# Hybrid attention block on one core: the projections between the heads as a stream of single products

## The chip, the cores and the metric

The kernel runs on one core of one Trainium2 chip. The metric is the device time of one execution in microseconds (us), the median of several runs. TensorE (PE in the profile) multiplies, VectorE (DVE), ScalarE (ACT) and GpSimd (POOL) work on rows, SyncE (SP) issues most transfers; each engine takes its instructions in a fixed order.

## The reference, cut to what matters

Two layers, each of an attention part and an MLP, on 512 rows of width 1024. In the attention part one normalised input `h` is projected, the projections go through four kinds of heads with four heads each, and the sixteen outputs go through `w_out`.

```
h = rmsnorm(x, norm_mix_g[l]) * (1.0 + sc1) + sh1
z = h @ w_in[l]
za, zb, zc, zd = split_last(z, [SWA_COLS, MLA_COLS, NSA_COLS, MOBA_COLS])
o = concatenate([swa_mixer(za), mla_mixer(zb), nsa_mixer(zc), moba_mixer(zd)])
x = x + g1 * (o @ w_out[l])
h = rmsnorm(x, norm_mlp_g[l]) * (1.0 + sc2) + sh2
x = x + g2 * (square(relu(h @ w_up[l])) @ w_down[l])
```

SWA is attention in a band of 128 keys with two key heads and a sink, MLA is causal attention over low-rank projections, NSA adds a compressed branch to two causal branches (at 512 rows all its blocks are chosen), MoBA is causal here too. Everything is in float32 and the output must agree with it.

## The kernel before, in words

**Products in three.** A float32 product is made of three single products of rounded operands (`fp32r`): weight high by input high, weight high by input low, weight low by input high (lines 363 to 369). The high part of a weight (`whi`, line 87) is made on ScalarE, the low part (`wlo`, line 91) on GpSimd. The class `Weights` hands weights out in the order in which they were added: `get` loads up to three weights ahead into four `raw` buffers (DMAs on SP), and splits up to three ahead into four pairs of buffers.

**Projections.** `proj_T` (line 394) makes one projection of 128 columns by 512 rows: for each of 8 blocks of depth three products of 512 columns into one PSUM bank, 24 in all, then an evacuation. `proj_N` (line 543) makes the values with the rows on the partitions: for MoBA (`proj_VB`) four banks, each of 24 products of 256 columns. A query evacuation (`q_evac`, line 506) is two copies on ScalarE and two subtractions on VectorE; a key evacuation (`k_evac`, line 519) is four copies on ScalarE (lines 525 and 526), two subtractions on VectorE and two copies on GpSimd.

**Heads.** `softmax` (line 581) takes four blocks of 128 queries: score products into one of two banks (`sc`), a fused add-and-minimum on VectorE (line 596), the exponential on ScalarE (line 601), the reciprocal, and the normalisation, for block 0 on GpSimd (lines 573, 575), for the others on ScalarE or VectorE. The rest of a head, its `tail`, is put on the list `pending` and traced by `flush` after the softmax of the next head. In the tail `pv` (line 616) transposes ten blocks of 128x128 (seven in an SWA head) on TensorE (line 626) in three groups of 4, 4 and 2 into PSUM tiles `pt`, of which there are two buffers. Each group is split into `ph` on ScalarE (line 448) and `pl` on VectorE (line 449), and then eight value products add into `po` (lines 641, 642).

**Order.** The heads come as four of MLA, eight of NSA (four heads, two branches), four of MoBA, four of SWA. Between the MLA heads stand two query projections of NSA (lines 869 and 913). Between the NSA and MoBA heads the list `fills` (lines 975 to 991) hands one closed projection to each head: the two key and two query projections of MoBA, its values, three empty places, then the key and two query projections of SWA. The output products (`px`) with `w_out` follow, and each may begin with the heads that are done.

The program order is no queue order. A planner reads the whole program, keeps a priority in program order, and gives each engine, by its own estimate of when an operand is ready, the first instruction that can go; so products of a later projection fill places where earlier work waits. `tc.issue_after(ins)` bars an instruction from being placed ahead of `ins` on its engine. `ada_step` puts one row product of the modulation on VectorE (line 191) and one load on SP behind each head, through the same `raw` buffers.

Of the kernel before, what the change touches and what calls it, by code (L numbers as in the profile page):

```python
# [11 lines left out]
F32R = mybir.dt.float32r  # L12
# [5 lines left out]
P = 128  # L18
S = 512
D = 1024  # L20
KT = D // P
# [7 lines left out]
NSTART = 5  # L29
# [80 lines left out]
def layer_stack(ctx: ExitStack, tc: tile.TileContext, a, out):  # L110
# [341 lines left out]
    def attention_layer(l, n1, finish):  # L452
# [25 lines left out]
        with ExitStack() as es:  # L478
# [79 lines left out]
                return ws  # L558


            pending = []

            def flush():
# [52 lines left out]
            def pv(po, vsrc, p, banks, first, last):  # L616

                prods = []
                for bi, bank in enumerate(banks):
                    pt = psT.tile([P, 512], F32, tag="pt", name="pt")  # L620
                    c = 0
                    spans = []
                    for j, qs in bank:
                        c0 = c
                        for n, col in qs:
                            nc.tensor.transpose(  # L626
                                pt[:, c : c + P], p[n][:, col : col + P], ident
                            )
                            c += P
                        spans.append((j, qs[0][0], c0, c))  # L630
                    wide = 256 if c <= 256 else 512
                    ph = sp.tile([P, wide], F32R, tag=f"ph{wide}", name=f"ph{bi}")[:, 0:c]
                    pl = sp.tile([P, wide], F32R, tag=f"pl{wide}", name=f"pl{bi}")[:, 0:c]
                    split(ph, pl, pt[:, 0:c])
                    for j, n0, c0, c1 in spans:
                        prods.append((j, n0 * P, ph[:, c0:c1], pl[:, c0:c1]))
                for i, (j, q0, ph, pl) in enumerate(prods):
                    w = ph.shape[1]
                    end = last and i == len(prods) - 1
                    dst, vhl = po[:, q0 : q0 + w], vsrc(j)  # L640
                    nc.tensor.matmul(dst, vhl, ph, start=(first and i == 0), stop=False)
                    nc.tensor.matmul(dst, vhl, pl, start=False, stop=end)
# [217 lines left out]
            mla_v(2)  # L860
            if l:
                proj_T(hs, [kcvc_evac])
            mla_head(1)
            ada_step(1, last["dve"])
            with tc.issue_after(last["dve"].ins):
                nc.vector.tensor_scalar_add(gates, gates, 1.0)
                nc.vector.reciprocal(gates, gates)
            if l or NSTART < 6:
                proj_T(hs, [q_evac(nq, 0)])

            cw2 = qp.tile([P, 192], F32, tag="cw2", name="cw2")
            nc.sync.dma_start(cw2, a["cw2"][l])
# [19 lines left out]
            for kv in range(2):  # L892
                nc.tensor.matmul(
                    hps[:, 32 * kv : 32 * kv + 32], hsb[:, kv * P : (kv + 1) * P], csum,
                    start=True, stop=True,
                )
            mla_head(2)
            ada_step(1, last["dve"])
            hx = qp.tile([P, 2, 31], F32, tag="hx", name="hx")
# [10 lines left out]
            nc.gpsimd.memset(grep, 0.0)  # L910
            nc.vector.tensor_copy(grep[:, :, 0:31], hx[:, 1:2, :].to_broadcast([P, 4, 31]))
            mla_q(3)
            proj_T(hs, [q_evac(nq, 1)])
            cps = mmbank("cmpkv")
            nc.tensor.matmul(cps[:, 0:31], cw2[:, 0:128], hx[:, 0, :], start=True, stop=True)
            nc.tensor.matmul(cps[:, 64:128], grep, cw2[:, 128:192], start=True, stop=True)
# [19 lines left out]
            split(vc[:, :, 0, :], vc[:, :, 1, :], vcf)  # L936

            biasN = [bias_tile("biasN", 0), bias_tile("biasN", 2)]
            mla_head(3)
            ada_step(1, last["dve"])  # L940

# [28 lines left out]
            nc.vector.tensor_tensor(ce_, ce_, cd.unsqueeze(2).to_broadcast([P, 16, 32]), op=ALU.mult)  # L970


            mq, mk, sq_, sk = {}, {}, {}, {}
            biasM, biasS = [], []
            fills = []

            def fill():
                if fills:
                    fills.pop(0)()

            def proj_VB():
                VB.append(xp.tile([P, NQ, 4, 2, 64], F32R, tag="V", name="VB"))
                proj_N(256, 4, lambda j, ps: v_evac(VB[0], j, ps, 4))

            VB = []
            for f in (k_evac(mk, 0), k_evac(mk, 1), q_evac(mq, 0), q_evac(mq, 1)):
                fills.append(lambda f=f: proj_T(hs, [f]))
            fills.append(proj_VB)
            fills += [lambda: None] * 3
            for f in (k_evac(sk, 0), q_evac(sq_, 0), q_evac(sq_, 1)):  # L990
                fills.append(lambda f=f: proj_T(hs, [f]))
            for h in range(4):
                pos_ = {}
                for br in range(2):
                    kh, kl = nk[br]

                    def scores(n, ps, kh=kh, kl=kl, h=h):
                        w = P * (n + 1)
                        qs = slice(n * P, n * P + P)
                        nc.tensor.matmul(ps, nq[h][:, qs], kh[:, 0:w], start=True, stop=False)  # L1000
                        nc.tensor.matmul(ps, nq[h][:, qs], kl[:, 0:w], start=False, stop=True)

                    gcol = 4 * (br + 1) + h
                    p = softmax(
                        scores, causal_w, rel(biasN[h // 2][:, h % 2, :]), -1.0, BIGPOS,
                        ("gate", lambda n, c=gcol: gates[:, n, c : c + 1]),
                    )
                    flush()

                    if h == br == 0:  # L1010
                        pct = psT.tile([P, 512], F32, tag="pt", name="pct")
                        for n in range(NQ):
                            nc.tensor.transpose(
                                pct[:, n * P : (n + 1) * P],
                                ce_[:, 4 * n : 4 * n + 4, :].rearrange("p h c -> p (h c)"), ident,
                            )
                        pch = mp.tile([P, S], F32R, tag="m", name="pch", bufs=8)
                        pcl = mp.tile([P, S], F32R, tag="m", name="pcl", bufs=8)
                        split(pch, pcl, pct)

                    def tail(h=h, br=br, p=p, pos_=pos_):
                        if br == 0:
                            pos_["po"] = psO.tile([P, 512], F32, tag="po", name="po")
                        po = pos_["po"]
                        pv(
                            po, lambda j: VA[:, j, 2 + br, :, :],
                            p, causal_banks, br == 0, False,
                        )
                        if br == 1:
                            nc.tensor.matmul(po, vc[:, h, :, :], pcl, start=False, stop=False)  # L1030
                            nc.tensor.matmul(po, vc[:, h, :, :], pch, start=False, stop=True)
                            o_evac(po, 2, h)
                            if h % 2:
                                o_done(4 + h // 2)
                    pending.append(tail)
                    fill()
                    ada_step(1, last["dve"])
                if h % 2:
                    biasM.append(bias_tile("biasM", h - 1))


            for h in range(4):
# [15 lines left out]
                    if h % 2:  # L1058
                        o_done(6 + h // 2)
                pending.append(tail)  # L1060
                fill()
                ada_step(1, last["dve"])
                if h == 1:
                    biasS.append(bias_tile("biasS", 0, 4, 256))


            nsink = smp.tile([P, 4], F32, tag="nsink", name="nsink")
# [325 lines left out]
```

## Time and profile before

| what | value |
|---|---|
| median of three runs | 1287.53 us (1287.36 to 1289.71) |
| the profiled execution | 1289.0 us |
| its span, first to last instruction | 1287.2 us |
| busy TensorE, VectorE, ScalarE, GpSimd | 97%, 53%, 45%, 42% |
| mean granted TensorE clock | 0.981 |
| attention heads, layer 0 and layer 1 | about 75 to 263 us, about 700 to 882 us |

A matmul's row in the trace gives its start and a modelled end that reaches over the start of the next one; the distance between two starts is what one of them costs. A bracket at the end of a row is the idle time of the engine before it and what ended it.

### The profile page before, as it was taken

The numbers are of one execution on the slowest core, as the hardware profiler recorded it, in microseconds if no ns is written. First come the engines' busy times: TensorE is split into PE (matmuls) and PEld (weight loads), VectorE is DVE, ScalarE is ACT, GpSimd is POOL, SyncE is SP. The second block draws the span as 40 slices with busy tenths as digits, with TensorE's granted clock in tenths as the row PEclk, the third lists the DMA queues.
The fourth block names the chain that finished last, engine by engine and source line by source line (L and its number), as shares of the span: only waits on it lengthen the run. The fifth ranks groups of instructions, "written<-read, shape, count | busy, mean of one in ns | idle before, by whom it ended". The sixth has DMA issues, their size and how long they took to land. (4 is left out here: it accounts for less than half of the span.)

```text
span 1287.2 us, 17945 instructions
## 1 busy us (share of the span) xinstructions
PE 1245.9 (97%) x6572; PEld 1042.1 (81%) x6572; DVE 681.3 (53%) x1498; ACT 583.4 (45%) x1121; POOL 545.8 (42%) x495
## 2 busy tenths in 40 slices
PE   5989999989999999999999999999999999999997
PEld 4878787879888888888899778778988888888887
DVE  5758867976455554553255685895543223123124
ACT  5557767744442231331245675884443223223120
POOL 5423323454645445445425432334364444444430
PEclk7989999999999999999999999999999999999998
DMA  9645324452366756655334411313142233323312
GB/s 339 246 118 164 115 72 142 148 201 90 120 191 204 243 183 224 222 182 199 126 110 140 135 43 57 99 58 107 50 131 89 93 98 98 98 85 95 99 33 66
DMA packets 53128, 171.02 MB, mean 133 GB/s; under 512 B 6192, under 2 KB 9776, under 8 KB 53040
## 3 DMA queue, kind: packets, MB, share of 16 engines
q1 hardware_dynamic: 51312, 165.67, 39.5%
q10 hardware_dynamic: 1728, 4.20, 1.0%
q8 instruction: 52, 0.85, 0.3%
q14 instruction: 36, 0.29, 0.1%
HBM read 163.29 MB, written 4.19 MB: 130 GB/s over the span
## 5 line engine op out<-in xcount | busy, mean ns | idle before, releaser
L91 POOL TENSOR_TENSOR wlo<-raw,whi 128x512 fp32r<-128x512 f32 (+3 forms) x372 | 488.2, 1337 | 560.8 <-ACT whi L87 525.3
L87 ACT ACTIVATE whi<-raw 128x1024 fp32r<-128x1024 f32 (+3 forms) x186 | 193.8, 1046 | 459.2 <-PE px L368 249.0
L368 PE MATMUL pj<-hlo,whi 128*128 128x512 f32 (+1 forms) x768 | 288.0, 376 | 0.0
L367 PE MATMUL pj<-hhi,whi 128*128 128x512 f32 (+1 forms) x768 | 287.1, 376 | 0.0
L369 PE MATMUL pj<-hhi,wlo 128*128 128x512 f32 (+1 forms) x768 | 287.1, 374 | 0.0
L367 PE MATMUL px<-a,whi 128*128 128x512 f32 (+2 forms) x584 | 214.9, 368 | 0.0
L368 PE MATMUL px<-a,whi 128*128 128x512 f32 (+2 forms) x584 | 214.7, 368 | 0.0
L369 PE MATMUL px<-a,wlo 128*128 128x512 f32 (+2 forms) x584 | 214.6, 368 | 0.0
L411 DVE SCALAR_TENSOR_TENSOR x<-px,mod,x 128x512 f32<-128x512 f32 (+2 forms) x95 | 62.7, 665 | 199.2 <-PE px L369 199.2
L369 PEld LDWEIGHTS pj<-hhi,wlo 128*128 128x128 f32 x768 | 144.9, 189 | 26.7
L368 PEld LDWEIGHTS pj<-hlo,whi 128*128 128x128 f32 x768 | 145.1, 189 | 26.1
L367 PEld LDWEIGHTS pj<-hhi,whi 128*128 128x128 f32 x768 | 144.1, 188 | 26.1
L191 DVE CUSTOM_DVE_ANT_0 adaw<-cb,adaw,vecs 128x1024 f32<-128x1024 f32 x78 | 102.0, 1307 | 50.7 <-DMA adaw<-in_wadaD 50.7
L368 PEld LDWEIGHTS px<-a,whi 128*128 128x128 f32 x584 | 109.7, 188 | 19.7
L367 PEld LDWEIGHTS px<-a,whi 128*128 128x128 f32 x584 | 109.7, 188 | 19.7
L369 PEld LDWEIGHTS px<-a,wlo 128*128 128x128 f32 x584 | 109.7, 188 | 19.7
L1134 DVE SCALAR_TENSOR_TENSOR t<-pj,r 128x512 f32<-128x512 f32 x64 | 44.1, 691 | 148.0 <-ACT r L1133 147.8
L449 DVE TENSOR_TENSOR a<-t,a 128x512 fp32r<-128x512 f32 x64 | 81.8, 1280 | 41.9 <-ACT a L448 41.9
L601 ACT ACTIVATE e<-e,nm 128x128 f32<-128x128 f32 (+5 forms) x160 | 85.9, 539 | 10.3 <-DVE nm L596 9.8
L449 DVE TENSOR_TENSOR pl<-pt,ph 128x512 fp32r<-128x512 f32 (+1 forms) x112 | 64.8, 597 | 5.9 <-ACT ph L448 5.1
L626 PE MATMUL pt<-ident,e 128*128 128x128 f32 x376 | 60.9, 276 | 4.3 <-POOL e L573 3.8
L448 ACT ACTIVATE ph<-pt 128x512 fp32r<-128x512 f32 (+1 forms) x112 | 56.0, 524 | 13.5 <-PE pt L626 12.2
(237 smaller groups left out, 1806.6 us busy)
## 6 DMA issues: line engine op xcount, KB each, us to landing
adaw<-in_wadaD SPq DMA_DIRECT2D x78, 512.0 KB, 4.4
raw<-in_wup SPq DMA_DIRECT2D x64, 512.0 KB, 3.6
raw<-in_wdown SPq DMA_DIRECT2D x64, 512.0 KB, 3.5
raw<-in_winT SPq DMA_DIRECT2D x28, 512.0 KB, 3.8
ada<-in_wadaP SPq DMA_DIRECT2D x16, 512.0 KB, 8.9
raw<-in_wout SPq DMA_DIRECT2D x16, 512.0 KB, 3.5
cw<-in_cw SPq DMA_DIRECT2D x4, 512.0 KB, 5.0
raw<-in_cw SPq DMA_DIRECT2D x4, 512.0 KB, 4.8
```

The lines of the kernel that those rows point to most:

```text
L87: self.nc.scalar.activation(vh[0:rows], raw[0:rows], AF.Copy)
L91: eng.tensor_tensor(lo[0:rows, c], flat[0:rows, c], hi[0:rows, c].bitcast(F32), op=ALU.subtract)
L191: last["ada"] = nc.vector.tensor_tensor_reduce(out=w, in0=cv, in1=w, scale=1.0, scalar=vecs[:, off : off + 1], op0=ALU.mult, op1=ALU.add, ...
L367: nc.tensor.matmul(ps, wh[:, k, :], hh[:, c], start=first, stop=False)
L368: nc.tensor.matmul(ps, wh[:, k, :], hl[:, c], start=False, stop=False)
L369: nc.tensor.matmul(ps, wl[:, k, :], hh[:, c], start=False, stop=last)
L411: last["dve"] = nc.vector.scalar_tensor_tensor(X["x"][m][:, c], ps, mod[l][:, part, m : m + 1], X["x"][m][:, c], op0=ALU.mult, op1=ALU.add)
L448: nc.scalar.activation(hi, src, AF.Copy)
L449: last["dve"] = nc.vector.tensor_tensor(lo, src, hi.bitcast(F32), op=ALU.subtract)
L601: nc.scalar.activation(ee, ee, AF.Exp, bias=nm[:, n : n + 1], scale=-1.0, accum_out=den[:, n : n + 1])
L626: nc.tensor.transpose(pt[:, c : c + P], p[n][:, col : col + P], ident)
L1134: nc.vector.scalar_tensor_tensor(t, ps, 0.0, r, op0=ALU.max, op1=ALU.mult)
```

## The change

The two query projections between the MLA heads and all projections of `fills` are no longer closed loops. `stream_T` and `stream_N` put their products one by one on a list, each with its number of columns; the first product of a bank draws the weight and the bank, the last one evacuates it. `pull` traces the next product. In `pv` each transposition is followed by one `pull`, and that product is tied behind the transposition by `issue_after`. After each NSA and MoBA head `fill(share)` traces untied products until the head's share is spent; `share` is a twelfth of all columns, 9216, the products pulled in `pv` count against it. `drain` traces what is left. The stream for the heads is made up before the last MLA head, so ten of its products are pulled there, and the three empty places are gone. What is computed stays the same.

```diff
@@ in attention_layer
+            stream, spent = [], [0.0, 0.0]
+            def pull(behind=None):
+                if not stream:
+                    return
+                cols, begin, product, end = stream.pop(0)
+                spent[0] += cols
+                if begin is not None:
+                    begin()
+                if behind is None:
+                    product()
+                else:
+                    with tc.issue_after(behind.ins):
+                        product()
+                if end is not None:
+                    end()
+            def drain():
+                while stream:
+                    pull()
+            def fill(cols):
+                spent[1] += cols
+                while stream and spent[0] < spent[1]:
+                    pull()
+            def stream_T(evac):
+                st = {}
+                def begin():
+                    st["w"], st["ps"] = W.get(), mmbank("pj")
+                for k in range(KT):
+                    for i, (a_, b_) in enumerate(((0, 0), (0, 1), (1, 0))):
+                        def product(k=k, i=i, a_=a_, b_=b_):
+                            nc.tensor.matmul(
+                                st["ps"], st["w"][a_][:, k, :], hs[k][b_],
+                                start=(k + i == 0), stop=(k == KT - 1 and i == 2),
+                            )
+                        stream.append((
+                            S, begin if k + i == 0 else None, product,
+                            (lambda: evac(st["ps"])) if k == KT - 1 and i == 2 else None,
+                        ))
+            def stream_N(ncols, step, evac):
+                st = {}
+                def begin(j):
+                    if j == 0:
+                        st["ws"] = [W.get() for _ in range(-(-KT // step))]
+                    st["ps"] = mmbank("pn")
+                for j in range(NQ):
+                    js = slice(j * P, (j + 1) * P)
+                    for k in range(KT):
+                        for i, (a_, b_) in enumerate(((0, 0), (0, 1), (1, 0))):
+                            def product(k=k, i=i, a_=a_, b_=b_, js=js):
+                                nc.tensor.matmul(
+                                    st["ps"][:, 0:ncols], hs[k][a_][:, js],
+                                    st["ws"][k // step][b_][:, k % step, :],
+                                    start=(k + i == 0), stop=(k == KT - 1 and i == 2),
+                                )
+                            stream.append((
+                                ncols, (lambda j=j: begin(j)) if k + i == 0 else None, product,
+                                (lambda j=j: evac(j, st["ps"])) if k == KT - 1 and i == 2 else None,
+                            ))
...
                         for n, col in qs:
-                            nc.tensor.transpose(
+                            pull(nc.tensor.transpose(
                                 pt[:, c : c + P], p[n][:, col : col + P], ident
-                            )
+                            ))
...
+            if l or NSTART < 6:
+                stream_T(q_evac(nq, 0))
             mla_head(1)
...
-            if l or NSTART < 6:
-                proj_T(hs, [q_evac(nq, 0)])
+            drain()
...
+            stream_T(q_evac(nq, 1))
             mla_head(2)
...
             mla_q(3)
-            proj_T(hs, [q_evac(nq, 1)])
+            drain()
...
+            mq, mk, sq_, sk = {}, {}, {}, {}
+            VB = []
+            def vb_evac(j, ps):
+                if j == 0:
+                    VB.append(xp.tile([P, NQ, 4, 2, 64], F32R, tag="V", name="VB"))
+                v_evac(VB[0], j, ps, 4)
+            for f in (k_evac(mk, 0), k_evac(mk, 1), q_evac(mq, 0), q_evac(mq, 1)):
+                stream_T(f)
+            stream_N(256, 4, vb_evac)
+            for f in (k_evac(sk, 0), q_evac(sq_, 0), q_evac(sq_, 1)):
+                stream_T(f)
+
+            share = sum(t[0] for t in stream) / 12
+            spent[:] = [0.0, 0.0]
             mla_head(3)
...
-            for f in (k_evac(mk, 0), k_evac(mk, 1), q_evac(mq, 0), q_evac(mq, 1)):
-                fills.append(lambda f=f: proj_T(hs, [f]))
-            fills.append(proj_VB)
-            fills += [lambda: None] * 3
-            for f in (k_evac(sk, 0), q_evac(sq_, 0), q_evac(sq_, 1)):
-                fills.append(lambda f=f: proj_T(hs, [f]))
...
-                    fill()
+                    fill(share)
...
-                fill()
+                fill(share)
...
+            drain()
```

## Rows read from the trace of the kernel before

**Rows 1.** The head of the page and its first part: busy time, share of the span and number of instructions by engine.

```profile
span 1287.2 us, 17945 instructions
PE 1245.9 (97%) x6572; PEld 1042.1 (81%) x6572; DVE 681.3 (53%) x1498; ACT 583.4 (45%) x1121; POOL 545.8 (42%) x495
```

**Rows 2.** Busy time by stretch: the stretch, its length, busy us of PE, PEld, DVE, ACT and POOL with the number of instructions, the granted clock of TensorE, the share of the DMA engines, GB/s. The first two are the heads of layer 0 from the first NSA head on, the fourth the NSA heads of layer 1, the third and the fifth are the MLP stages.

```profile
119.00:193.00 74.00, 71.82 (x427) 60.64 (x426) 57.56 (x182) 53.25 (x130) 18.68 (x22) 1.00 0.30 92
193.00:232.00 39.00, 36.32 (x185) 29.01 (x183) 31.59 (x90) 29.45 (x71) 15.04 (x14) 0.96 0.46 150
...
300.00:672.00 372.00, 371.01 (x1804) 308.91 (x1804) 186.34 (x284) 120.04 (x168) 179.13 (x134) 1.00 0.54 177
...
745.00:810.00 65.00, 63.07 (x371) 52.17 (x371) 45.31 (x141) 44.10 (x105) 20.35 (x22) 1.00 0.16 51
...
920.00:1287.00 367.00, 359.39 (x1711) 297.39 (x1711) 108.14 (x158) 107.73 (x146) 155.84 (x124) 0.99 0.27 86
```

**Rows 3.** The waits of TensorE over the whole span: what waited, for whom, us in total, times, the longest.

```profile
PE po L641 <- ACT ph L448: 6.5, 13, 2.3
...
PE pt L626 <- POOL e L573: 3.8, 1, 3.8
...
PE px L367 <- ACT ohi L448: 1.5, 1, 1.5
```

**Rows 4.** The timeline of TensorE around four transpositions in a run (first four rows) and around a single one between products of 512 columns (last three rows): start, us, line, operation, how many were merged.

```profile
132.01 0.39 PE L1001 MATMUL sc<-kl,q 128*128 128x512 f32 x1
132.24 0.60 PE L626 MATMUL pt<-ident,e 128*128 128x128 f32 x4
...
132.91 0.40 PE L369 MATMUL pj<-hhi,wlo 128*128 128x512 f32 x1
133.14 0.40 PE L367 MATMUL pj<-hhi,whi 128*128 128x512 f32 x1
...
90.35 0.40 PE L842 MATMUL sc<-mkh,mql 128*128 128x512 f32 x1
90.58 0.27 PE L626 MATMUL pt<-ident,e 128*128 128x128 f32 x1
...
90.92 0.39 PE L368 MATMUL pj<-hlo,whi 128*128 128x512 f32 x1
```

**Rows 5.** The MoBA heads of layer 0: the timeline of TensorE (first three rows), of ScalarE (two rows), and the stretch at the lower clock (columns as in Rows 2).

```profile
210.56 0.50 PE L641 MATMUL po<-ph,VB 128*128 128x512 f32 x1 [2.30 <-ACT ph L448]
...
213.17 0.63 PE L368 MATMUL pj<-hlo,whi 128*128 128x512 f32 x1
213.59 0.63 PE L369 MATMUL pj<-hhi,wlo 128*128 128x512 f32 x1
...
204.27 1.06 ACT L87 ACTIVATE whi<-raw 128x1024 fp32r<-128x1024 f32 x1 [1.72 <-DMA raw<-in_wout]
...
209.91 1.09 ACT L448 ACTIVATE ph<-pt 128x512 fp32r<-128x512 f32 x2
...
212.10:215.50 3.40, 3.40 (x13) 2.92 (x11) 1.62 (x3) 0.70 (x2) 0.00 (x0) 0.50 0.76 193
```

**Rows 6.** The end of the heads of layer 0: the timeline of TensorE (two rows), and the group of the first third of the output products between 73 and 263 us (line, engine, operation, shape, count, busy us, mean ns, idle before).

```profile
265.98 1.20 PE L367 MATMUL px<-ohi,whi 128*128 128x512 f32 x4 [1.55 <-ACT ohi L448]
...
269.94 0.50 PE L369 MATMUL px<-ohi,wlo 128*128 128x512 f32 x1 [0.49 <-POOL wlo L91]
...
L367 PE MATMUL px<-ohi,whi 128*128 128x512 f32 x28 | 11.2, 405 | 0.2
```

**Rows 7.** The timeline of TensorE in the NSA heads of layer 1, from the second transposition group to the third.

```profile
768.32 0.71 PE L626 MATMUL pt<-ident,e 128*128 128x128 f32 x5
768.78 0.48 PE L367 MATMUL pj<-hhi,whi 128*128 128x512 f32 x1
...
772.27 0.39 PE L367 MATMUL pj<-hhi,whi 128*128 128x512 f32 x1
773.19 0.50 PE L641 MATMUL po<-ph,VA 128*128 128x512 f32 x1 [0.52 <-ACT ph L448]
...
774.22 0.38 PE L626 MATMUL pt<-ident,e 128*128 128x128 f32 x2
```

**Rows 8.** The timeline of ScalarE in the same stretch: the split of a weight, the first and the last of the four copies of a key evacuation, and the split of the transposed blocks.

```profile
766.42 1.06 ACT L87 ACTIVATE whi<-raw 128x1024 fp32r<-128x1024 f32 x1 [1.39 <-PE pj L368]
767.38 0.58 ACT L525 ACTIVATE kh<-pj 64x512 fp32r<-64x512 f32 x1
...
770.21 0.60 ACT L526 ACTIVATE kh<-pj 64x512 fp32r<-64x512 f32 x1
...
772.54 1.08 ACT L448 ACTIVATE ph<-pt 128x512 fp32r<-128x512 f32 x2
```

**Rows 9.** The second MLA head of layer 0: one row each of the timelines of TensorE, of ScalarE and of GpSimd, and the stretch at the lower clock (columns as in Rows 2).

```profile
84.22 0.48 PE L626 MATMUL pt<-ident,e 128*128 128x128 f32 x1 [3.77 <-POOL e L573]
...
79.95 1.06 ACT L87 ACTIVATE whi<-raw 128x1024 fp32r<-128x1024 f32 x1 [2.72 <-DMA raw<-in_winT]
...
81.08 2.49 POOL L91 TENSOR_TENSOR wlo<-raw,whi 128x512 fp32r<-128x512 f32 x2 [5.07 <-ACT whi L87]
...
82.40:89.20 6.80, 4.98 (x17) 4.30 (x18) 3.53 (x13) 3.28 (x11) 2.10 (x3) 0.50 0.35 99
```

More of the change, by code (lines that the diff above doesn't have):

```diff
@@ L970, in attention_layer @@
             nc.vector.tensor_tensor(ce_, ce_, cd.unsqueeze(2).to_broadcast([P, 16, 32]), op=ALU.mult)
-            mq, mk, sq_, sk = {}, {}, {}, {}
             biasM, biasS = [], []
[L975 to L985, printed above, removed]
-            for f in (k_evac(mk, 0), k_evac(mk, 1), q_evac(mq, 0), q_evac(mq, 1)):
-                fills.append(lambda f=f: proj_T(hs, [f]))
-            fills.append(proj_VB)
-            fills += [lambda: None] * 3
-            for f in (k_evac(sk, 0), q_evac(sq_, 0), q_evac(sq_, 1)):
-                fills.append(lambda f=f: proj_T(hs, [f]))
             for h in range(4):
```

## The prediction

> **What bounds the kernel now.** I read the shares by engine first: TensorE is busy 1245.9 of 1287.2 us, 97% [rows 1]. So time can only come from the 41 us in which TensorE stands still, from stretches at its lower clock, or from a lower price of its own work. Then the stages: in the head stages TensorE is busy 71.82 of 74, 36.32 of 39 and 63.07 of 65 us, with VectorE and ScalarE at 68 to 81% beside it [rows 2]; the reader is to see that three engines are nearly full there and hand work round in a circle (scores, exponential, transposition, split, value product). Then the waits of TensorE: a value product waits for the split `ph` 13 times, 6.5 us, one of 2.3 us; one transposition waits 3.8 us for a row block normalised on GpSimd; an output product waits 1.5 us for a split [rows 3]. The MLP stages, nearly three fifths of the span, hold no line of the change and stay as they are.
>
> The sum is made against the profiled execution, 1289.0 us, which is its span of 1287.2 and 1.8 around it. It lies 1.5 us above the median of 1287.53; the same difference taken from the median is the forecast. About 0.2% of it, 2.6 us, is what can be told from no change.
>
> **The change part by part.** *Count of work.* Per layer the stream carries 24 + 24 + 7 x 24 products of 512 columns and 96 of 256; before they were the same products in closed loops. Nothing is added or removed, so TensorE's own work changes only if a transposition between products has another price than one in a run. In a run: from the score product at 132.01 to the second product after four transpositions, at 132.91, is 0.90 us; two products at 0.23 (132.91 to 133.14) leave 0.44, so 0.110 each. Alone: 90.35 to 90.92 is 0.57 us; less 0.46 leaves 0.11 [rows 4]. Same price, so 0 us.
>
> The Trainium skill (TensorE: Matmul & The Clock Gate, the steps of a matmul and LDWEIGHTS) says that a weight load is pulled ahead of the product in flight and takes its columns over 1.2 ns, some 107 ns by estimate. By that a transposition between two long products would hide its load; the lone one above does not show the gain, since the product behind it has only the short transposition to load its own weights under.
>
> *What is tied.* 15 tails of a layer (MLA 0 to 3, NSA 0 to 7, MoBA 0 to 2) find a filled stream, with 10 transpositions each: 150 products a layer stand behind a given transposition. After them a head gets the rest of its share, 9216 columns: 8 products of 512 free of any tie. In the kernel before all 24 of a projection were free filler.
>
> *Waits for `ph`.* Twelve of the 13 are 4.2 us together [rows 3]. Behind each first transposition bank there now always stand some products, whatever the planner thought of ScalarE's speed; against that, the heads' evacuations come at other places. Between 0 and -4.2; I take the middle, -2.1.
>
> *The stall in the MoBA heads, layer 0.* TensorE stands 2.30 us to 210.56, and then products are 0.42 us apart instead of 0.23: the granted clock of 212.1 to 215.5 is 0.50, the 1.2 GHz level, after the engine had idled. Half of 3.4 us is 1.7, so 4.0 in all [rows 5]. Its root is ScalarE, whose queue stood 1.72 us before the split of a `wout` weight that had not landed, with `ph` behind it only at 209.91. After the change the two projections before that weight are drawn head by head and not as early as the planner can, so the load is asked for at another point. Between 0 and -4.0; I take three quarters, -3.0, since this ordering must be met exactly to recur.
>
> *The end of the heads, layer 0.* TensorE stands 1.55 and 0.49 us at 265.98 and 269.94, when the output products have nothing left but the last head's own; 28 of each third of these products were used as filler before 263 [rows 6]. The stream now lasts into the fourth MoBA head, so fewer are spent there. Between 0 and -2.0; I take -1.5.
>
> *A new tie.* The score transposition banks are two. The third bank's two transpositions wait until the first bank's split has read it. Row: five transpositions from 768.32, the next two at 774.22; in the 4 us between, 16 products stood before the first value product, and even so it waited 0.52 [rows 7]. After the change products 9 and 10 are tied to those last two, and all later ones of the same projection follow in order, so this filler is locked just there. In most heads the split comes soon and the four products behind transpositions 5 to 8 (0.9 us) and two score blocks of the next head (0.46) cover it. The exception is NSA head 1 in both layers: the stream began in MLA 3 with 10 and NSA 0 with 10, so the first MoBA key projection ends behind the fourth transposition, and its four `kh` copies (0.6 each) enter ScalarE ahead of `ph` [rows 8]. The second MoBA key projection and the SWA one end outside a bank or behind transposition 6, with `ph` of the first bank already ahead. Per layer between 0 (`ph` slips in first, the copies wait) and 4.0 (5.4 us from 768.78 to 774.22, less 1.4 of cover), plus 1.7 if the clock falls. I take +1.5, nearer to the 0.52 that such a burst leaves now than to the full price: +3.0 for both.
>
> *Fetches and queues.* A weight is now drawn at its first product, so its DMA on SP, its `whi` on ScalarE and `wlo` on GpSimd enter up to a head earlier; numbers and sizes are unchanged, the queues are held by free raw buffers, and TensorE's cover hides them. What it costs if that cover is gone is seen at 84.22: `whi` waited 2.72 us for its load, `wlo` held GpSimd 2.49 us, the row block came late and TensorE idled 3.77 us [rows 9], with 5 us at half clock behind it (about 2.5). This stall lies ahead of the first tied product and its causes are not moved, so I leave it: 0, with -6.2 if it goes and +1.5 if the three products that may no longer fill between its late transpositions are missed.
>
> Sum: 0 - 2.1 - 3.0 - 1.5 + 3.0 + 0 = -3.6 us, 1285.4 for the profiled execution, 1283.9 beside the median: **1284 us**.
>
> **The rivals.** *The lock is dear (slower).* ScalarE takes the four copies before `ph` in NSA head 1, TensorE stands 3.0 us and falls to the lower clock for 1.7, in both layers: +9.4 in place of +3.0; and the MoBA stall only moves, as the SWA key projection's copies make one like it: 0 in place of -3.0. Sum -2.1 - 1.5 + 9.4 = +5.8, 1293 us. For it: each key evacuation now leaves a wait even with 16 products of cover [rows 7, 8]. Against it: the copies end before `ph` only if the planner finds them ready first. It decides from a lock of about 3 us a layer, where the gains are eaten.
>
> *The stalls move (same).* Lock of 2.5 a layer without the clock: -6.6 + 5.0 = -1.6, 1286 us. For it: VectorE and ScalarE at 68 to 81% [rows 2], so a few idle microseconds of TensorE are theirs wherever products stand.
>
> *A transposition hides its load (much faster).* If one between products costs a quarter of a 512-column product, 0.058 instead of 0.110, 300 save 0.052 each, 15.6 us: with the rest about 1268. The lone one in [rows 4] speaks against it; the skill's pull-ahead, cited above, is the rule that would give it.
>
> *The 84 us stall goes too.* -3.6 - 6.2: 1278 us. Against it: the late load is not moved.
>
> That the change does not do what it says would show as products away from transpositions: the tie only bars a product from going ahead, so the planner may still put one later.
>
> **How the numbers follow.** Forecast 0.33 (own range 1280 to 1285), the 84 us stall gone as well 0.06, hidden loads 0.03: faster by over 0.2%, 0.42. Stalls move, 1285 to 1290: 0.26. Lock dear: 0.32, 1290 to 1300. The range is 1276 to 1296: it leaves out hidden loads and a part of the 84 us case below, and a tenth above, where the lock falls at full price with the clock in both layers.
>
> **What would show it.** Right: transpositions alternate with `pj` products, the distance over a pair stays 0.34 us; no wait of 2 us before a value product in the MoBA heads; output products still unspent at the end of SWA. Wrong: TensorE waits over 2 us in NSA head 1 for `ph` or for a transposition behind `pl`, with clock 0.50 after it; or a pair at 0.29. A new wait at a load on ScalarE's queue would say that the moved fetches, which I cost at nothing, decide.

## The result and the profile after

The changed kernel is slower: 1305.63 us (median of 4 runs, 1302.63 to 1310.81) against 1288.62 for the kernel before (4 runs, 1287.36 to 1290.24) on the same chip. The ratio is 1.0129 [1.0105, 1.0153], so some 17 us. The profiled execution took 1305.32 us with a span of 1303.4, 16.2 longer than before. The forecast was 1284 with a range of 1276 to 1296.

First the head of the page, against [rows 1]:

```profile
span 1303.4 us, 17939 instructions
PE 1250.4 (96%) x6572; PEld 1039.4 (80%) x6572; DVE 688.4 (53%) x1498; ACT 586.1 (45%) x1121; POOL 543.5 (42%) x495
```

TensorE runs the same 6572 matmuls. It is busy only 4.5 us longer; the other 11.7 of the 16.2 us are idle time. Next the waits of TensorE over the span (what waited, for whom, us in total, times, longest), against [rows 3]:

```profile
PE pt L698 <- DVE pl L449: 4.8, 7, 2.0
PE po L713 <- ACT ph L448: 4.7, 10, 1.3
...
PE sc L1120 <- DVE nm L668: 3.4, 2, 2.9
PE sc L1072 <- DVE nm L668: 2.6, 2, 2.1
...
PE pt L698 <- POOL e L645: 1.2, 1, 1.2
```

Two of the old waits shrank: for `ph` from 6.5 to 4.7 us, near the forecast, and for the late row block on GpSimd from 3.8 to 1.2, which the forecast had left as it was. The two largest new waits are a transposition behind the split `pl` (4.8 us) and score products behind `nm`, VectorE's row maximum (6.0 us together). They come with projection products still unspent. The longest of each, 1.97 and 2.93 us, have a second cause, a late load, which is taken up below.

How one of them arises is seen in the timeline of TensorE, in an NSA head of layer 0 (the tail of the third). Here a pair of transposition and product comes first, the last pair of the second group follows, and then what stands before the third group:

```profile
147.25 0.27 PE L698 MATMUL pt<-ident,e 128*128 128x128 f32 x1
147.28 0.48 PE L599 MATMUL pj<-hhi,whi 128*128 128x512 f32 x1
147.60 0.27 PE L698 MATMUL pt<-ident,e 128*128 128x128 f32 x1
147.62 0.48 PE L599 MATMUL pj<-hlo,whi 128*128 128x512 f32 x1
...
149.07 0.44 PE L1072 MATMUL sc<-kh,q 128*128 128x384 f32 x1 [0.51 <-DVE nm L668]
...
149.75 0.40 PE L1073 MATMUL sc<-kl,q 128*128 128x512 f32 x1
151.47 0.50 PE L713 MATMUL po<-ph,VA 128*128 128x512 f32 x1 [1.32 <-ACT ph L448]
...
152.58 0.30 PE L698 MATMUL pt<-ident,e 128*128 128x128 f32 x1 [0.62 <-DVE pl L449]
152.64 0.48 PE L599 MATMUL pj<-hhi,wlo 128*128 128x512 f32 x1
```

The eighth transposition is at 147.60, the ninth at 152.58. Between them the engine has one tied product, eight score products and one value product, and it idles 0.51, 1.32 and 0.62 us. No `pj` product stands in the gap after 147.62: the next one is tied to the ninth transposition, which waits for `pl`. On ScalarE two key copies and three passes over `e` (two of them not shown) go ahead of the split in that time:

```profile
148.39 0.59 ACT L525 ACTIVATE kh<-pj 64x512 fp32r<-64x512 f32 x1
148.99 0.59 ACT L526 ACTIVATE kh<-pj 64x512 fp32r<-64x512 f32 x1
...
149.99 0.71 ACT L673 ACTIVATE e<-e,nm 128x512 f32<-128x512 f32 x1
...
150.82 1.08 ACT L448 ACTIVATE ph<-pt 128x512 fp32r<-128x512 f32 x2
```

The same place in the next head has no key copy near it, but a query copy goes ahead of the split on ScalarE (third row):

```profile
160.25 0.49 PE L713 MATMUL po<-ph,VA 128*128 128x512 f32 x1 [0.64 <-ACT ph L448]
...
161.66 0.33 PE L698 MATMUL pt<-ident,e 128*128 128x128 f32 x1 [0.92 <-DVE pl L449]
...
158.98 0.59 ACT L512 ACTIVATE q<-pj 64x512 fp32r<-64x512 f32 x1
159.60 1.09 ACT L448 ACTIVATE ph<-pt 128x512 fp32r<-128x512 f32 x2
```

The longest wait for `pl`, two heads later, looks alike and is another thing. Ten products of the value projection (`pn`) did run in front of it, the last at 178.60, and VectorE stood behind a late load of `adaw` (a row of the modulation weights) with `pl` behind it in its queue:

```profile
178.60 0.28 PE L622 MATMUL pn<-whi,hhi 128*128 128x256 f32 x1
180.85 0.33 PE L698 MATMUL pt<-ident,e 128*128 128x128 f32 x1 [1.97 <-DVE pl L449]
...
178.16 1.28 DVE L191 CUSTOM_DVE_ANT_0 adaw<-cb,adaw,vecs 128x1024 f32<-128x1024 f32 x1 [2.08 <-DMA adaw<-in_wadaD]
```

Behind some of the larger stalls the granted clock falls to 0.50, the 1.2 GHz level. Four such stretches (columns as in [rows 2]):

```profile
181.70:185.10 3.40, 3.40 (x15) 3.21 (x14) 2.12 (x5) 0.73 (x2) 0.00 (x0) 0.50 0.17 67
202.20:205.60 3.40, 3.27 (x9) 2.56 (x10) 2.81 (x8) 2.59 (x9) 2.77 (x3) 0.50 0.08 13
792.70:796.10 3.40, 3.40 (x13) 3.01 (x12) 2.94 (x13) 2.36 (x7) 0.45 (x1) 0.50 0.24 93
297.80:304.50 6.70, 6.70 (x31) 6.70 (x32) 1.63 (x5) 1.67 (x3) 3.35 (x4) 0.50 0.43 131
```

The first stands behind the 1.97 us wait above, the second behind waits in a MoBA head, the third behind one of 2.14 us for `nm` in layer 1. The fourth lies after the heads and is taken up below: other versions have it too.

### The profile page after: what moved, and what is told of

Its sections match the earlier page's. It is cut to its first block, busy times and chain, and to the rows that moved or that the text cites. A ratio compares the mean times of both kernels' runs of the same rounds, so it can differ in the third digit from the quotient of the medians.

```text
span 1303.4 us, 17939 instructions
## 1 busy us (share of the span) xinstructions
PE 1250.4 (96%) x6572; PEld 1039.4 (80%) x6572; DVE 688.4 (53%) x1498; ACT 586.1 (45%) x1121; POOL 543.5 (42%) x495
## 5 line engine op out<-in xcount | busy, mean ns | idle before, releaser
L368 PE MATMUL pj<-hlo,whi 128*128 128x512 f32 (+1 forms) x624 | 229.9, 369 | 0.0
L369 PE MATMUL pj<-hhi,wlo 128*128 128x512 f32 (+1 forms) x624 | 229.1, 368 | 0.0
L367 PE MATMUL pj<-hhi,whi 128*128 128x512 f32 (+1 forms) x624 | 228.7, 369 | 0.0
L191 DVE CUSTOM_DVE_ANT_0 adaw<-cb,adaw,vecs 128x1024 f32<-128x1024 f32 x78 | 104.7, 1343 | 57.6 <-DMA adaw<-in_wadaD 57.6
L368 PEld LDWEIGHTS pj<-hlo,whi 128*128 128x128 f32 x624 | 117.2, 188 | 22.1
L369 PEld LDWEIGHTS pj<-hhi,wlo 128*128 128x128 f32 x624 | 117.2, 188 | 22.0
L367 PEld LDWEIGHTS pj<-hhi,whi 128*128 128x128 f32 x624 | 116.5, 188 | 21.9
L698 PE MATMUL pt<-ident,e 128*128 128x128 f32 x376 | 90.9, 277 | 6.0 <-DVE pl L449 4.8
L599 PE MATMUL pj<-hhi,whi 128*128 128x512 f32 x144 | 64.8, 450 | 0.0
```

The source lines that it names most:

```text
L191: last["ada"] = nc.vector.tensor_tensor_reduce(out=w, in0=cv, in1=w, scale=1.0, scalar=vecs[:, off : off + 1], op0=ALU.mult, op1=ALU.add, ...
L367: nc.tensor.matmul(ps, wh[:, k, :], hh[:, c], start=first, stop=False)
L368: nc.tensor.matmul(ps, wh[:, k, :], hl[:, c], start=False, stop=False)
L369: nc.tensor.matmul(ps, wl[:, k, :], hh[:, c], start=False, stop=last)
L599: nc.tensor.matmul(st["ps"], st["w"][a_][:, k, :], hs[k][b_], start=(k + i == 0), stop=(k == KT - 1 and i == 2),)
L698: pull(nc.tensor.transpose(pt[:, c : c + P], p[n][:, col : col + P], ident))
```

## The experiments

None of the kernels leaves work out. Ratios are to the kernel before on the same chip, with the 95% interval. In the expectations A says that the ties lock the filler, and B that the equal shares (the draining per head) cost the time. A1 and A2 differ over how much of A goes through the third group of transpositions, which must wait for one of two PSUM tiles. C and D set the ties themselves against the modulation weights that arrive late.

**e1 and e11: the streams without ties.** Every product is still drawn at the same place in the program, one per transposition, but the planner may put it earlier.

```diff
-                if behind is None:
-                    product()
-                else:
-                    with tc.issue_after(behind.ins):
-                        product()
+                product()
```

> The products are pulled in the same program order, but none is tied behind its transposition. Theory A (the tie locks the filler: behind the third group of transpositions, which waits for a PSUM tile, nothing of the stream may run): most of the 16 us goes away, 1286 to 1293 us, and the waits of transpositions for pl, 4.8 us after, fall below 1.5. Theory B (the equal shares: 18 products a head instead of 24, so ScalarE and VectorE set the pace of every head): it stays at 1300 to 1307.

Measured 1286.66 us, ratio 0.9968 [0.9945, 0.9991]. Repeated in five rounds as e11:

> The kernel without ties once more, to say whether it is faster than the kernel before: 1283 to 1288 us, a ratio of 0.995 to 0.999. If the first reading was chance: within 0.2% of the kernel before.

1287.43 against 1290.47, ratio 0.9973 [0.9960, 0.9986]. So 1305.63 - 1286.66 = 19 us come back with this edit alone (20 if each is set against the kernel before in its own rounds: 17.0 slower, 3.0 faster), and what is left is 3 us faster than before. B falls: the shares are the same here. The waits of transpositions for `pl` fell to 0.8 us in e1, as A expected, but only to 2.6 in e11, where 1.9 of it is the late load's. In e1's timeline of TensorE the place between the second and the third group looks like this:

```profile
146.93 0.27 PE L694 MATMUL pt<-ident,e 128*128 128x128 f32 x1
146.95 0.48 PE L595 MATMUL pj<-hlo,whi 128*128 128x512 f32 x1
147.27 0.40 PE L595 MATMUL pj<-hhi,wlo 128*128 128x512 f32 x1
147.50 0.40 PE L595 MATMUL pj<-hhi,whi 128*128 128x512 f32 x1
147.73 0.39 PE L709 MATMUL po<-ph,VA 128*128 128x512 f32 x1
147.97 0.40 PE L595 MATMUL pj<-hlo,whi 128*128 128x512 f32 x1
...
148.90 0.39 PE L595 MATMUL pj<-hhi,wlo 128*128 128x512 f32 x1
149.13 0.38 PE L694 MATMUL pt<-ident,e 128*128 128x128 f32 x2
```

Eight `pj` products stand between the groups, nothing waits, and the ninth transposition comes 2.2 us after the eighth, where it took 5.0. The 1.97 us wait, however, has its match here, without any tie (in e11 it is 1.86, for `pl`):

```profile
175.97 0.44 PE L694 MATMUL pt<-ident,e 128*128 128x128 f32 x2 [2.11 <-DVE rc L646]
```

Two windows, from the first score product of a layer's heads to the broadcast of the norm behind their output, show the cost by layer; the first two rows are the changed kernel's (layer 0, layer 1), the next fence is e1's:

```profile
73.10:315.40 242.30, 220.57 (x1294) 180.81 (x1294) 178.58 (x498) 156.24 (x365) 80.35 (x90) 0.97 0.40 129
710.50:936.60 226.10, 217.47 (x1318) 181.15 (x1318) 159.92 (x469) 148.25 (x349) 78.71 (x92) 0.99 0.26 84
```

```profile
76.40:304.50 228.10, 212.00 (x1294) 176.89 (x1294) 177.33 (x498) 155.74 (x365) 82.47 (x90) 0.99 0.43 137
699.00:917.40 218.40, 213.77 (x1319) 179.87 (x1319) 156.24 (x469) 147.01 (x349) 78.68 (x92) 1.00 0.27 87
```

With ties layer 0's stretch is 14.2 us longer and layer 1's 7.7. The spans differ by 18.9 only, because e1 came to its first score product 3.3 us later (76.40 against 73.10), after a stretch at clock 0.50 (59.5 to 66.2) that lies ahead of the heads. Idle time of TensorE is 5.6 and 4.0 us of the two (242.30 - 220.57 less 228.10 - 212.00, and so on). The rest, 8.6 and 3.7, is time in which the engine was busy with the same number of matmuls (but for one). About 5 and 1.7 us of that, by estimate, are the lower clock: layer 0 has 13.5 us at 0.50 in the fence above and e1 3.4 (from 284.7), layer 1 has 3.4 and e1 none, and about half of such a stretch is lost (0.42 us a product instead of 0.23 [rows 5]). The remaining 3.5 and 2 stay open.

Not all of the 14.2 us is the ties' either. Up to the start of TensorE's wait for the broadcast after the heads (294.99 and 288.80) the difference is 9.5; the other 4.7 come with that wait and the clock behind it, which differ between executions of one program (last section). Of the 9.5, the MLA heads have 3.4. The rows go from the first score product to the first transposition of the third tail, with the same matmuls in all (kernel before, changed kernel, e1):

```profile
76.18:114.44 38.26, 34.26 (x224) 27.73 (x224) 26.39 (x74) 24.77 (x56) 12.81 (x14) 0.91 0.48 155
73.06:109.36 36.30, 34.57 (x224) 26.07 (x224) 26.22 (x74) 25.15 (x56) 13.14 (x14) 1.00 0.49 149
76.36:109.23 32.87, 31.72 (x224) 25.83 (x224) 25.64 (x74) 24.86 (x56) 12.86 (x14) 1.00 0.51 164
```

There the stream gains 5.4 us untied and 2.0 tied, at full clock in both; 2.9 of the 3.4 between them are busy time of TensorE, and why is not shown.

**e3: the shares alone.** The transpositions draw nothing; each head draws its whole share at its end.

```diff
-                            pull(nc.tensor.transpose(
+                            nc.tensor.transpose(
                                 pt[:, c : c + P], p[n][:, col : col + P], ident
-                            ))
+                            )
```

> No transposition pulls a product; each head gets its equal share behind its tail as free filler. Theory A: the ties are the loss, so this is near the kernel before, 1284 to 1291 us. Theory B: the shares are the loss, 1297 to 1306.

1293.89 us, ratio 1.0019 [1.0002, 1.0037]: 3 us above A's range and 3 below B's. Shares without products behind the transpositions cost at most a little, and this run had a stall of 4.2 us in the second MLA head, the one of [rows 9]. B as the main cause falls a second time.

**e2, e6 and e7: which ties.** The groups have four, four and two transpositions. e2 draws (and ties) only behind the first two groups, e6 ties only behind the third, e7 only behind the first:

```diff
-                            pull(nc.tensor.transpose(
+                            t = nc.tensor.transpose(
...
-                            ))
+                            )
+                            pull(t if bi == 2 else None)
```

This is e6; e7 has `bi == 0`, and e2 has `if bi < 2: pull(t)` in its place.

> Only the transpositions of the first two groups of a tail pull a tied product; the third group, which waits for a free PSUM tile, pulls none, so 10 instead of 8 products of a share are free once the eighth transposition is through. Theory A: if the lock is at the third group, most goes away, 1287 to 1295 us. Theory B, or a tie that harms at every transposition: 1299 to 1306.

> Every transposition pulls a product, but only the two of the third group of a tail, which wait for a free PSUM tile, tie theirs. If the lock at the third group is a loss by itself: 1292 to 1298 us, with waits of transpositions for pl above 2 us in sum. If the ties harm only together with those of the first eight: 1285 to 1290, as without ties.

> Every transposition pulls a product, but only the four of the first group tie theirs. If only the third group locks: 1285 to 1289 us, as without ties. If a tie locks wherever the planner would have drawn the stream ahead of the tail: 1290 to 1298, as with ties at the first eight (1298 less a share).

| what is tied, per head | time, us | ratio [95%] |
|---|---|---|
| nothing (e11) | 1287.43 | 0.9973 [0.9960, 0.9986] |
| first group, 4 (e7) | 1290.90 | 1.0024 [1.0006, 1.0041] |
| first two, 8; third draws none (e2) | 1298.47 | 1.0064 [1.0044, 1.0085] |
| third group, 2 (e6) | 1295.92 | 1.0064 [1.0046, 1.0082] |
| all 10 (the change) | 1305.63 | 1.0129 [1.0105, 1.0153] |

From no tie to the two of the third group is 0.9 points of ratio, and as much to the eight of the first two. So the two ties behind the tile wait are the dearest for their number, but the lock is not theirs alone. e2 lies above A's range and just under B's: most of the loss did not go away. e6 lies in the range of a lock at the third group, but not with the sign that was named for it: its transpositions wait only 1.1 us for `pl`, and score products wait 6.4 for `nm`, where e1 has 0.9. In e6 the MLA stretch above takes 33.0 us, as without ties, and in e7 35.7; the loss in the MLA heads belongs to the ties of the earlier groups.

**e9 and e10: a third tile for the transposed blocks,** with and without ties. The PSUM tile is taken from the projections, which keep two (the MLP's first banks are counted out accordingly).

```diff
-    psA = ctx.enter_context(tc.tile_pool(name="psA", bufs=3, space=PSUM))
-    psT = ctx.enter_context(tc.tile_pool(name="psT", bufs=2, space=PSUM))
+    psA = ctx.enter_context(tc.tile_pool(name="psA", bufs=2, space=PSUM))
+    psT = ctx.enter_context(tc.tile_pool(name="psT", bufs=3, space=PSUM))
```

> The changed kernel, ties and all, with three PSUM tiles for transpositions instead of two (and two banks for projections instead of three, two projections instead of three in the heads of the MLP stages). The third group of a tail no longer waits for the split of the first. To be read against the next run, the same without ties. Theory A1 (the lock at the third group is the wait for its tile): the difference between the two falls from 19 us to 8 to 13, and waits of transpositions for pl nearly vanish. Theory A2 (ties harm whatever the tiles): the difference stays at 16 to 22. The level of both is open, since the projections have a bank less: 1285 to 1325.

> The same three tiles, with the products pulled in the same order and no tie. Theory A1: 8 to 13 us under the run before it. Theory A2: 16 to 22 us under it. Against the kernel before: 1283 to 1305 us, by what the missing bank costs.

1303.47 us tied, 1.0100 [1.0082, 1.0118], and 1297.33 untied, 1.0059 [1.0039, 1.0079]. With three tiles the ties cost 6.1 us instead of 19, less than either theory had (8 to 13, 16 to 22). The wait of transpositions for `pl`, 4.8 us and 7 times in the changed kernel, is in e9:

```profile
PE pt L698 <- DVE pl L449: 0.8, 1, 0.8
```

The wait for the tile has thus nearly gone, but the pair does not say how much of the lock it was. The difference shrank mostly because the untied kernel became 10 us slower (1287.43 to 1297.33), the tied one only 2 faster (1305.63 to 1303.47). The projections have a bank less in both, and that too may keep the untied stream from running ahead; this rival was not tested. The share of the third group is better read from e6, where nothing else changes.

**e4, e5 and e8: the MLA heads.** e4 streams and ties in the MLA heads and gives the other heads their list of closed loops back; e5 is the reverse; e8 streams everywhere and ties only until the share is computed, that is in the tails drawn before.

```diff
 e4, behind each NSA and MoBA head
-                    fill(share)
+                    give()
 e5, around the MLA heads
-            stream_T(q_evac(nq, 1))
...
-            drain()
+            proj_T(hs, [q_evac(nq, 1)])
 e8
-                if behind is None:
+                if behind is None or not tie[0]:
...
             share = sum(t[0] for t in stream) / 12
+            tie[0] = False
             spent[:] = [0.0, 0.0]
```

> The two query projections between the MLA heads are streamed and tied as in the changed kernel; the list of closed projections for the NSA and MoBA heads is as before. Both theories put the loss into the NSA and MoBA heads: 1282 to 1290 us, and with the 84 us stall of layer 0 (6.2 us with its lower clock) gone as in the changed kernel nearer to 1283. If the MLA part harms as well, 1291 or more.

> The complement of the run with the MLA streams alone: the two projections between the MLA heads are closed loops as before, the NSA and MoBA heads are streamed and tied as in the changed kernel. If the parts add up, the changed kernel's loss plus the 2 us that the MLA part gained: 1304 to 1310 us, with the 84 us stall of layer 0 back. If the loss needs both parts, under 1300.

> Ties behind the transpositions of the first two MLA heads alone, none in the NSA and MoBA heads, which pull in the same order. If the small gains of the MLA streams with ties and of the untied heads add up: 1283 to 1286 us, faster than the kernel before by 0.2 to 0.4%. If the untied stream had both already: 1286 to 1288.

e4: 1287.13 us, 0.9981 [0.9962, 1.0001]. e5: 1313.30, 1.0207 [1.0185, 1.0229], which is 7.7 us above the whole change and 3 above the range for parts that add up. The MLA part is a gain, even with its ties, and its place is the stall of [rows 9]. e5 (first row) has it again, the changed kernel (second fence) does not:

```profile
83.50 0.33 PE L698 MATMUL pt<-ident,e 128*128 128x128 f32 x1 [3.67 <-DVE rc L678]
```

```profile
78.29 0.33 PE L698 MATMUL pt<-ident,e 128*128 128x128 f32 x1 [1.21 <-POOL e L645]
```

e8 missed: 1291.34 us, 1.0021 [1.0002, 1.0041], where 1283 to 1288 was expected. Its twelve executions lie between 1284.3 and 1295.7, and the profiled one is the slowest of them. Its MLA stretch, with ties as in the changed kernel, takes 36.4 us against 32.9 in e1:

```profile
75.65:112.07 36.42, 34.56 (x225) 26.07 (x225) 26.22 (x74) 25.27 (x56) 13.15 (x14) 1.00 0.50 150
```

So ties cost 3.5 us in the MLA heads alone, a good part of the 0.5 points of ratio by which e8 lies above e1 and e11. That gains of two parts add up is not borne out.

**e12 and e13: the modulation weights moved.** In the changed kernel VectorE's queue stands behind a late load of `adaw`, and with it the row maxima that the scores wait for:

```profile
218.69 1.28 DVE L191 CUSTOM_DVE_ANT_0 adaw<-cb,adaw,vecs 128x1024 f32<-128x1024 f32 x1 [3.38 <-DMA adaw<-in_wadaD]
```

```profile
220.37 0.45 PE L1120 MATMUL sc<-kh,q 128*128 128x384 f32 x1 [2.93 <-DVE nm L668]
```

So the row products were taken out from behind the NSA and MoBA heads (they follow later), with ties (e12) and without (e13):

```diff
                     fill(share)
-                    ada_step(1, last["dve"])
...
                 fill(share)
-                ada_step(1, last["dve"])
```

> The changed kernel with ties, but the row products of the modulation behind the NSA and MoBA heads of layer 0, and their loads, are left to the end of the heads. VectorE then never stands before such a load inside those heads (10.5 us after). Theory C (the late loads, 5 us of TensorE's waits, are a part of the tie's loss): the difference from the next run, the same without ties, falls from 18 us to 9 to 14. Theory D (the loss is the lock before the third group and the heads' own chain): the difference stays at 15 to 20. The level moves by what the row products cost at the end, 10 of 1.3 us: 1298 to 1315.

> The same without ties. Theory C: 9 to 14 us under the run before it. Theory D: 15 to 20 us under it. Against the kernel before: 1284 to 1300 us.

1300.81 us, 1.0097 [1.0072, 1.0122], and 1284.03, 0.9961 [0.9945, 0.9977]. The ties still cost 16.8 us, in D's range. But the edit did not take the late loads out of the heads altogether. In e12 a row product still stands in the MoBA heads, with a score product behind it as before:

```profile
214.09 1.29 DVE L191 CUSTOM_DVE_ANT_0 adaw<-cb,adaw,vecs 128x1024 f32<-128x1024 f32 x1 [3.69 <-DMA adaw<-in_wadaD]
...
215.77 0.44 PE L1119 MATMUL sc<-kh,q 128*128 128x384 f32 x1 [3.25 <-DVE nm L668]
```

So the pair does not say what the late loads are worth. The traces bound it: in the changed kernel such loads stand behind two waits of TensorE, 1.97 us, which e1 has too, and 2.93, which it has not; the latter is 3 of the 19 at most. In the stretches of layer 0 VectorE waits for `adaw` just as long in the changed kernel (10.5 us, 6 times) as in e1 (10.4, 7 times). The load behind the 2.93 us has its match in e1, where VectorE waits 2.68 us and TensorE has no wait of 0.15 us or more between 208.2 and 219.0, since it had products to fill with:

```profile
213.20 1.28 DVE L191 CUSTOM_DVE_ANT_0 adaw<-cb,adaw,vecs 128x1024 f32<-128x1024 f32 x1 [2.68 <-DMA adaw<-in_wadaD]
```

e13 is the fastest kernel here, though its interval overlaps that of e11.

## Why the prediction was wrong, step by step

**"Count of work": right.** Over the pairs of the heads the distance from one transposition to the next with a 512-column product between has a median of 0.345 us (173 pairs), with a 256-column one 0.231 (32). That is 0.23 + 0.11 and no gain below a product, so the rival of the hidden load falls. The Trainium skill's pull-ahead (TensorE: Matmul & The Clock Gate, the steps of a matmul and LDWEIGHTS) would by the prediction's price have given 0.29 a pair; the shortest pair in the trace takes 0.339. Nor does the change fail to do what it says: a transposition is followed by a projection product 274 times, and by another transposition 73 times, 262 before.

**"Waits for `ph`": right in size** (-1.8 measured, -2.1 forecast), but read by itself: the waits for `pl` and `nm` of the same chain are 10.8 us (4.9 of them behind the late loads), where the kernel before had under 1.

**"The stall in the MoBA heads": right that it goes, wrong that its time is won.** No value product waits 2 us for `ph` any more, with ties or without (e1's longest is 1.4). In the tied kernel the 2.93 us stall at 220.37 takes its place; e1 has no wait for `nm` above 0.7, but one of 1.8 for an output tile in those heads.

**"The end of the heads": mis-sized.** 1.55 us became 1.09 with ties and up to 1.6 without, so about -0.5 at most for -1.5.

**The 84 us stall, costed at 0: wrong.** It shrank from 3.77 us with low clock behind it to 1.21 at full clock, some 5 us. Of the sentence "This stall lies ahead of the first tied product and its causes are not moved" the second half failed. The weight that came late before (`whi` waited 2.72 us for it) is there in time now, and ScalarE goes on to it without a wait:

```profile
73.51 0.59 ACT L886 ACTIVATE mkh<-mk 64x512 fp32r<-64x512 f32 x1
74.00 1.05 ACT L87 ACTIVATE whi<-raw 128x1024 fp32r<-128x1024 f32 x1
```

The wait is short, 1.0 to 1.4 us, in all the runs whose MLA tails draw the stream, e1 without ties among them, and long in the two whose MLA tails draw none (4.2 in e3, 3.7 in e5).

**"A new tie", +3.0: the step that failed.** It measured 19 us. All the other terms together were forecast at -6.6 and measured -3.0 twice (e1, e11), so they were within 4 us; this one was wrong by 16. That the others came so near is partly luck: the MLA part, costed at 0, is -2.6 by itself in e4, so the three forecast gains brought next to nothing in sum, as far as parts add up. The mechanism was named: products behind a late transposition are locked, and all later ones with them. What failed is the sentence "in most heads the split comes soon and the four products behind transpositions 5 to 8 (0.9 us) and two score blocks of the next head (0.46) cover it". Cover was 1.4 us, and the stretch from the eighth to the ninth transposition is 5.0 us in the timeline above. Nor was it confined to the one head that was named. In NSA head 1 of layer 0 two key copies did go ahead of `ph`, and TensorE waited only 0.23 us (131.94). The stall above came two heads later, where copies of the second MoBA key projection went ahead of `ph`; the prediction had excluded that. In the head after it (160.25, 161.66) a query copy was enough. The term left out the MLA heads as well, where the ties cost 3.4 us and "+1.5 if the three products [...] are missed" stood beside a cost of 0. [Rows 7] showed it: 16 products stood between the groups before the change and even so the value product waited 0.52, while the new kernel allows one. I read that wait of 0.52 as the price of the place, when the 16 products were its cover, to be taken away in every head. The bounds, 0 to 5.7 a layer, were drawn for one head a layer and therefore too narrow.

**The rivals.** "The lock is dear" had the right sign and the right mechanism, but its place, NSA head 1, was not the one, and its price was half of what was measured (9.4 for 19), again because it counted one head per layer. "The stalls move" names something real (the MoBA stall) that decides nothing.

**"What would show it".** The sign of a wrong forecast, a wait of over 2 us in NSA head 1 with clock 0.50 after it, is not there; later NSA heads have waits for `pl` of 0.62 and 0.92 us, and the one with the lower clock behind it (1.97) is the late load's. Two signs of a right forecast are there: transpositions alternate with `pj` products at 0.345 us, and no value product of the MoBA heads waits 2 us. So the signs looked at single places, where the loss was spread over many.

## What to carry to other kernels

An order edge that holds filler behind an instruction of the critical chain takes from it what makes it filler: when that instruction waits, the product tied to it waits too, and the rest of its projection behind it (147.62 to 152.64 above). Draw such products one by one at the places where they are wanted, but leave the planner free to run them early; here that was worth 19 us in 1306, and the untied stream beat both the closed loops and the tied stream. When a tie is costed, count the products that stand in each gap in the trace before, not the wait that is left after them.

## What the hardware showed that was not expected

The same idle time did not always cost the same. The 1.97 us wait to 180.85 is followed by 3.4 us at the lower clock from 181.7, while after the 2.93 us to 220.37 the granted clock of 220.3 to 224.0 is 1.00, and so it is in e1 (177 to 181) after the 2.11 us to 175.97. What sets the difference is open.

One stall belongs to no version: the broadcast of the row sums after the heads (`rsb`, behind VectorE's `sqacc`) waited 1.7 us before, 2.8 after, 1.1 in e1 and 2.5 in e11, which is the same program as e1. In the changed kernel 6.7 us at half clock follow it, so it lends one profiled execution some 3 us that another doesn't have; the medians, not the profiles, carry the verdicts.
